# The sample's indexer on both halves of the partitions, its head sums in one bank

## The chip, the cores and the metric

The program runs on one core of a Trainium2 chip. The metric is the device time of one execution in microseconds (us), the median of three runs: 1997.98 us before (1997.33 to 1998.3). The engines are called by their names in the profile: PE (TensorE's products), PEld (its weight loads), DVE (VectorE), ACT (ScalarE), POOL (GpSimd) and SP, whose queue issues nearly all DMAs.

## The reference, cut to what matters

One layer of a decoder for two groups of requests with shared weights: a prompt of 1024 tokens, and a sample of 8 sequences with 8 new tokens each and 512 past keys in pages of 128. The indexer scores each key for each token; the best ones are then attended. The change touches only the indexer of the sample:

```
def select_attend(q, qi, wi, q_pos, k_all, v_all, ki_all):
    ...
    dots = jnp.einsum('bthd,bld->bthl', qi.astype(jnp.float32), ki_all.astype(jnp.float32))
    score = jnp.einsum('bth,bthl->btl', wi.astype(jnp.float32), jax.nn.relu(dots)) * IDX_SCALE
    score = jnp.where(causal[None], score, -jnp.inf)
    _, idx = lax.top_k(score, n_sel)
    ...
```

For one sequence of the sample that is 8 heads x 8 tokens = 64 queries of 64 numbers against 520 keys (512 past, 8 new), a relu, and a weighted sum over the heads, which leaves 8 x 520 scores.

## The kernel before, in words

The whole kernel is one program, written by a planner (the class `Weaver`). The parts of the work are generators ("streams"). The main stream is a long row of projections in fp32r, three products for each 128 x 128 piece of a weight: `pj<-h_hi,wh`, `pj<-h_lo,wh`, `pj<-h_hi,wl`. At each `yield` the planner picks which stream goes on, by its own estimate of each engine's time, so the order of every engine's instructions is fixed when the program is built. A change in one stream moves the others too.

Side streams that run between the projections of the first 350 us:

- `score_stream`: the prompt's indexer, blocks `qb` 2 to 7. A head's chunk of 512 keys is two products (`at<-ki_hi,qstk`, `at<-ki_lo,qstk`), a relu on ACT into one of two buffers (`relu`), and a multiply-add on DVE into `scores` (0.75 us for 512 columns).
- `samp_idx`: the sample's indexer, sequence by sequence. `fetch(b)` reads four page numbers into registers on SP and issues four loads of 128 x 64 keys (`kraw_i`). Four transposes bring them to `pt`, an ACT copy to `kidxT` (64 partitions x 520), and a small DVE copy appends the 8 new keys from `kis`. Two fp32 products of 260 columns (`at<-kidxT,qis`, 64 rows x 64 columns of the array), each with a relu into `srelu`, then two head sums of 260 columns (`at<-srelu,xt`, 64 rows x 8 columns) with an ACT copy each into `sb`, and a DMA of `sb` to its 8 rows of `score_s`. An fp32 product is two PE instructions in the trace.
- `search`: the threshold search on DVE over finished scores, step by step, and after both indexers are done (`scores_done`, the event `ev_go`) the attention of the prompt, `attn`. The sample's own attention, `samp_attn`, follows at about 805 to 905 us.
- `rope` is the rotary step on DVE behind each projection of q, k and the indexer: one product with the cosine table (`rt<-pj,cos`) and two with the sine table (`ru<-pj,sin`); POOL adds the two. Ahead of the first key projection the tables are loaded anew for heads of 128 (`pre_tab(128)`, `load_tabs`): two DMAs of 128 x 1088 floats, `cos<-c_cos` and `sin<-c_sin`, in SP's queue.

Tags are rings of buffers that the planner counts: PSUM banks `pj` (3), `at` (2), `pt` (2), `po` (1); SBUF tiles `M`, `K1`, `Z`, `p`, `S`. An instruction that waits for another engine holds up what the program has behind it on its own.

Of the kernel before, what the change touches and what calls it, by code (L numbers as in the profile page):

```python
# [11 lines left out]
F32 = mybir.dt.float32  # L12
# [16 lines left out]
IH, ID = 8, 64  # L29
PAST, PAGE = 512, 128  # L30
NPG = PAST // PAGE
LS = PAST + NQ
# [22 lines left out]
def n_prompt(c):  # L55
    c0, n = CH[c]
    return min(n, SEQ - c0)
# [258 lines left out]
def hybrid_decoder_step(ctx, tc, I, O):  # L316
    nc = tc.nc
    W = Weaver(nc)
    ctx.enter_context(tc.manual_schedule())

    def dram(shape, dtype, name):
        return tc.dram_tile(shape, dtype, name=name)
# [5 lines left out]
    qis_scr = dram([IH * ID, NS], F32, "qis_scr")  # L328
# [10 lines left out]
    const = ctx.enter_context(tc.tile_pool(name="const", bufs=1))  # L339
# [32 lines left out]
    kis = const.tile([ID, NS], F32, name="kis")  # L372
    ones = const.tile([P, P], F32, name="ones")
    ptab = const.tile([1, NB * NPG], I32, name="ptab")

# [252 lines left out]
    tpool = att.enter_context(tc.tile_pool(name="att", bufs=1, reuse_waits="tile"))  # L628
# [3 lines left out]
    tM = tagged(tpool, "M", 5)  # L632
    tK = tagged(tpool, "K1", 6)
    tZ = tagged(tpool, "Z", 2)
# [215 lines left out]
    def evac_ki(c, ps):  # L850
        c0, n = CH[c]
        npr = n_prompt(c)
        if c == 0:
            st["kh"] = tp_([P, SEQ], F32R, name="ki_hi")
            st["kl"] = tp_([P, SEQ], F32R, name="ki_lo")
        t, u = rope(ps, c, 32, 64)
        W.act(t[64:72, :n], ps[64:72, :n], AF.Copy, n)
        free_ps()
        W.spawn(ki_parts(c, t, u))

    def ki_parts(c, t, u):
# [12 lines left out]
        W.tt(kl[64:128, c0:c0 + npr], t[0:64, :npr], src, OP.subtract, npr)  # L874
        ev_ki[c].t = W.cur.t
        if npr < n:
            W.act(kis, t[0:64, npr:n], AF.Copy, NS)
        W.spawn(ki_out(c, t))

    def ki_out(c, t):  # L880
        yield {"pt": 1, "S": 1}
        ps = psum("pt")
        tl = tok_tiles(c)
        for j, (i, m) in enumerate(tl):
            W.tr(ps[:m, j * 72:(j + 1) * 72], t[:72, j * P:j * P + m], ident[:72, :72])
# [12 lines left out]
        W.later(store)  # L898
# [497 lines left out]
    def pages(b):  # L1396
        W.issue = max(W.issue, W.cur.t) + 2.2
        return [nc.sync.value_load(ptab[0:1, b * NPG + n:b * NPG + n + 1], min_val=0, max_val=I["n_phys"] - 1) for n in range(NPG)]

    def page(cache, v):  # L1400
        return cache[bass.ds(v, 1)].rearrange("o t d -> (o t) d")

    def samp_idx():
        yield ev_wi[2]
        for m in range(4):
            yield ev_qi[m][2]
        yield {"Z": 2, "K1": 1}
        qraw = tZ([ID, IH, NS], name="qis_raw")
        qis = tZ([ID, NB, IH, NQ], name="qis")
        W.load(qraw, qis_scr.rearrange("(h d) t -> d h t", d=ID))  # L1410
        W.go("pool", 2.0)
        nc.gpsimd.tensor_copy(qis.rearrange("p b h q -> p h b q"), qraw.rearrange("p h (b q) -> p h b q", q=NQ))
        W.give("Z")
        xw = tK([NS, IH, NQ], name="xw")
        W.go("dve", 0.2)
        nc.vector.tensor_tensor(xw, wi_c[:NS, 8, :].unsqueeze(2).to_broadcast([NS, IH, NQ]),
                                sdelta.unsqueeze(1).to_broadcast([NS, IH, NQ]), op=OP.mult)
        yield {"pt": 1}
        ps = psum("pt")
        W.tr(ps[:NS, :NS], xw.rearrange("p h q -> p (h q)"), ident[:NS, :NS])  # L1420
        W.give("K1")
        xt = tpool.tile([NS, NS], F32, name="xt")
        W.act(xt, ps[:NS, :NS], AF.Copy, NS)
        W.give("pt")
        yield None
        kr = {}

        def fetch(b):
            yield {"K1": 1}
            kr[b] = tK([P, NPG, ID], name="kraw_i")  # L1430
            t = W.cur.t
            for n, v in enumerate(pages(b)):
                t = W.dma(kr[b][:, n, :], page(I["ckidx"], v))
            kr[b] = (kr[b], t + 3.0)
        yield from fetch(0)
        for b in range(NB):
            if b + 1 < NB:
                yield from fetch(b + 1)
            k_, t = kr.pop(b)
            W.cur.t = max(W.cur.t, t)  # L1440
            yield {"pt": 1, "M": 2}
            ps = psum("pt")
            for n in range(NPG):
                W.tr(ps[:ID, n * P:(n + 1) * P], k_[:, n, :], ident)
            W.give("K1")
            kT = tM([ID, LS], name="kidxT")
            r = tM([NS, LS], name="srelu")
            W.act(kT[:, :PAST], ps[:ID, :], AF.Copy, 512)
            W.give("pt")
            W.ts(kT[:, PAST:LS], kis[:, b * NQ:(b + 1) * NQ], 1.0, None, OP.mult, None, NQ)  # L1450
            yield None
            for a in (0, 260):
                yield {"at": 1}
                ps = psum("at")
                W.mm(ps[:NS, :260], qis[:, b, :, :].rearrange("p h q -> p (h q)"), kT[:, a:a + 260], 260, True, True, f32=True)
                t0 = W.cur.t
                W.act(r[:, a:a + 260], ps[:NS, :260], AF.Relu, 260)
                W.give("at")
                t1, W.cur.t = W.cur.t, t0
            W.cur.t = t1  # L1460
            W.give("M")
            yield {"M": 1}
            sb = tM([NQ, LS], name="sb")
            for a in (0, 260):
                yield {"at": 1}
                ps = psum("at")
                W.mm(ps[:NQ, :260], xt[:, b * NQ:(b + 1) * NQ], r[:, a:a + 260], 260, True, True, f32=True)
                t0 = W.cur.t
                W.act(sb[:, a:a + 260], ps[:NQ, :260], AF.Copy, 260)
                W.give("at")  # L1470
                t1, W.cur.t = W.cur.t, t0
            W.give("M")
            W.cur.t = t1
            yield None
            W.store(score["s"][b * NQ:(b + 1) * NQ, :], sb)
            W.give("M")
        W.give("Z")
        W.cur.t += 2.5
# [577 lines left out]
    M = {}  # L2056
# [419 lines left out]
```

## Time and profile before

| what | value |
|---|---|
| median of three runs | 1997.98 us (1997.33 to 1998.3) |
| the profiled execution: its own time | 1997.44 us |
| its span in the profile | 1995.7 us |
| PE busy | 1944.2 us, 97% of the span |
| DVE, ACT, POOL busy | 64%, 36%, 37% |
| mean granted clock of TensorE | 0.989 |

So 1.74 us of the profiled execution's time lie outside its span, and it is 0.54 us under the median. The shares are averages over stages: PE is full nearly everywhere, DVE is nearly full from about 205 to 500 us and half idle before. A busy share of PE counts a product from its start to its modelled end, and products overlap, so two starts in a row tell more than a duration.

### The profile page before, as it was taken

How to read it: one execution, taken by the hardware profiler on the slowest of the kernel's cores; microseconds unless marked ns; L12 is line 12 of the kernel's file. 1: busy time of each engine (PE TensorE's matmuls, PEld its weight loads, DVE VectorE, ACT ScalarE, POOL GpSimd, SP SyncE). 2: the span in 40 equal slices, each digit the busy share in tenths (PEclk: the TensorE clock that was granted, in tenths of full speed). 3: DMA queues.
4: the chain of work that ended last, by engine and by line, in shares of the span. 5: the costliest groups of instructions: out<-in, count | busy, mean ns of one | idle time of the engine just before them, and what ended most of it. 6: DMA issues, size and time to landing. Idle time of an engine off the chain costs nothing.

```text
span 1995.7 us, 36382 instructions
## 1 busy us (share of the span) xinstructions
PE 1944.2 (97%) x13585; PEld 1864.6 (93%) x13585; DVE 1277.0 (64%) x2727; ACT 713.1 (36%) x1448; POOL 742.7 (37%) x661
## 2 busy tenths in 40 slices
PE   8998999999999999999999899999999999999998
PEld 6987879999999999779999899999999999999988
DVE  6635899899988896323438776566666653314754
ACT  5354443312433325433334532232232322213543
POOL 2533445323223242214444233232232354424873
PEclk9999999999999999999999899999999999999999
DMA  4664325222222222446453332222222343212343
GB/s 151 177 192 110 107 83 151 65 56 73 78 73 55 56 64 72 125 118 187 127 157 113 131 95 86 66 81 81 71 79 79 122 151 106 91 43 85 105 152 96
DMA packets 291243, 205.27 MB, mean 103 GB/s; under 512 B 28448, under 2 KB 270680, under 8 KB 291066
## 3 DMA queue, kind: packets, MB, share of 16 engines
q1 hardware_dynamic: 290822, 202.85, 34.1%
q8 instruction: 107, 1.75, 0.4%
q14 instruction: 70, 0.57, 0.1%
q10 hardware_dynamic: 244, 0.09, 0.0%
HBM read 151.43 MB, written 51.31 MB: 102 GB/s over the span
## 4 chain that ended last, share of the span: by engine, by line
PE 81%; DVE 5%; POOL 2%; issue 2%; DMA 1%; ACT 1%; DVEq 0%; SPq 0%; POOLq 0%; ACTq 0%
PE pj L154 42%; PE pj L190 27%; PE at L186 5%; PE po L186 4%; PE pt L197 3%; POOL wl L150 1%; DVE scores L139 1%; DVE ru L135 0%; DMA q_hi<-ple_scr 0%; POOL x L150 0%; DVE junk L1225 0%; DVE x L135 0%; POOL whl L150 0%; DVE q_lo L135 0%; PE at L197 0%
## 5 line engine op out<-in xcount | busy, mean ns | idle before, releaser
L150 POOL TENSOR_TENSOR wl<-wraw,wh 128x512 fp32r<-128x512 f32 (+2 forms) x233 | 298.9, 1286 | 651.1 <-ACT wh L131 642.1
L190 PE MATMUL pj<-h_hi,wh 128*128 128x384 f32 (+2 forms) x1197 | 406.6, 340 | 0.3 <-ACT wh L131 0.3
L190 PE MATMUL pj<-h_hi,wl 128*128 128x384 f32 (+2 forms) x1197 | 393.6, 329 | 0.7 <-POOL wl L150 0.7
L190 PE MATMUL pj<-h_lo,wh 128*128 128x384 f32 (+2 forms) x1197 | 393.3, 329 | 0.0
L131 ACT ACTIVATE wh<-wraw 128x512 fp32r<-128x512 f32 (+2 forms) x233 | 141.5, 610 | 279.7 <-PE pj L154 137.6
L190 PEld LDWEIGHTS pj<-h_hi,wh 128*128 128x128 f32 (+1 forms) x1197 | 225.9, 189 | 16.3 <-issue 12.4
L190 PEld LDWEIGHTS pj<-h_lo,wh 128*128 128x128 f32 (+1 forms) x1197 | 226.1, 189 | 2.5
L190 PEld LDWEIGHTS pj<-h_hi,wl 128*128 128x128 f32 (+1 forms) x1197 | 225.4, 188 | 1.8 <-POOL wl L150 1.1
L154 PE MATMUL pj<-f_hi,whl 128*128 128x272 f32 x1056 | 206.0, 288 | 0.0
L154 PE MATMUL pj<-f_hi,wl 128*128 128x272 f32 x704 | 203.6, 289 | 0.5 <-DVE wl L135 0.5
L154 PE MATMUL pj<-f_hi,wh 128*128 128x272 f32 x704 | 203.3, 289 | 0.0
L154 PE MATMUL pj<-f_lo,wh 128*128 128x272 f32 x704 | 202.6, 288 | 0.0
L154 PE MATMUL pj<-m_hi,wh 128*128 128x272 f32 x644 | 186.2, 289 | 1.0 <-ACT tha L131 0.5
L154 PE MATMUL pj<-m_hi,wl 128*128 128x272 f32 x644 | 185.9, 289 | 0.0
L154 PE MATMUL pj<-m_lo,wh 128*128 128x272 f32 x644 | 185.8, 289 | 0.0
L135 DVE TENSOR_TENSOR x<-pj,x 128x272 f32<-128x272 f32 x160 | 69.5, 437 | 173.6 <-PE pj L154 170.5
L154 PEld LDWEIGHTS pj<-f_hi,whl 128*128 128x128 f32 x1056 | 168.8, 189 | 0.0
L154 PE MATMUL pj<-f_lo,whl 128*128 128x272 f32 x528 | 152.4, 289 | 0.0
L154 PEld LDWEIGHTS pj<-f_hi,wl 128*128 128x128 f32 x704 | 132.9, 189 | 0.7 <-DVE wl L135 0.7
L154 PEld LDWEIGHTS pj<-f_hi,wh 128*128 128x128 f32 x704 | 132.8, 189 | 0.0
L154 PEld LDWEIGHTS pj<-f_lo,wh 128*128 128x128 f32 x704 | 132.7, 189 | 0.0
L154 PEld LDWEIGHTS pj<-m_hi,wh 128*128 128x128 f32 x644 | 121.4, 188 | 1.5 <-ACT tha L131 0.8
(364 smaller groups left out, 4566.9 us busy)
## 6 DMA issues: line engine op xcount, KB each, us to landing
wraw<-in_w_in SPq DMA_DIRECT2D x112, 256.0 KB
wraw<-in_w_gate_up SPq DMA_DIRECT2D x92, 256.0 KB
wraw<-in_w_down SPq DMA_DIRECT2D x40, 256.0 KB
wraw<-in_w_out SPq DMA_DIRECT2D x32, 256.0 KB
wraw<-in_w_ple_gate SPq DMA_DIRECT2D x32, 256.0 KB
x<-in_x_prompt SPq DMA_DIRECT2D x13, 512.0 KB
m_scr<-q_hi SPq DMA_DIRECT2D x18, 272.0 KB
q_lo<-m_scr SPq DMA_DIRECT2D x18, 272.0 KB
```

Source lines behind the costliest of these rows:

```text
L131: self.nc.scalar.activation(out, in_, func, **kw)
L135: self.nc.vector.tensor_tensor(out, a, b, op=op)
L139: self.nc.vector.scalar_tensor_tensor(out, a, s, b, op0=op0, op1=op1)
L150: self.nc.gpsimd.tensor_tensor(out, a, b, op=op)
L154: self.nc.tensor.matmul(ps, l, r, start=start, stop=stop)
L186: self.nc.tensor.matmul(ps, l, r, start=start, stop=stop)
L190: self.nc.tensor.matmul(ps, l, r, start=start, stop=stop)
L197: self.nc.tensor.transpose(ps, in_, ident)
```

## The change

The sample's keys are laid on all 128 partitions: transposes of two pages at a time (128 x 128) put pages 0 and 1 on partitions 0 to 63 and pages 2 and 3 on partitions 64 to 127 (the page order in `kraw_i` is changed for that), so `kidxT` is 128 x 264, with the 8 new keys behind both halves (`kis` and the queries `qis` now stand on both halves, too). The two fp32 products of a sequence now have 264 columns each and different quarters of the array: rows and columns 0 to 63, and rows and columns 64 to 127. They write the two halves of one `at` bank, and one relu takes both. The weights of the head sum, `xt`, are spread with zeros to 64 columns for each sequence (a POOL memset and two ACT copies, once), so that the sums of all eight sequences add up in one `po` bank, `acc`, by quarters as before; it is copied to `score_s` once at the end by two ACT copies. The copies to `sb` and the eight DMAs to `score_s` are gone.

```diff
@@ ki_parts
         if npr < n:
-            W.act(kis, t[0:64, npr:n], AF.Copy, NS)
+            for e in range(2):
+                W.act(kis[e * ID:(e + 1) * ID, :], t[0:64, npr:n], AF.Copy, NS)
@@ samp_idx
-        W.load(qraw, qis_scr.rearrange("(h d) t -> d h t", d=ID))
+        for e in range(2):
+            W.load(qraw[e * ID:(e + 1) * ID], qis_scr.rearrange("(h d) t -> d h t", d=ID))
...
+        xt = tZ([P, NB * NS], name="xt")
+        W.go("pool", 0.7)
+        nc.gpsimd.memset(xt, 0.0)
...
-            for n, v in enumerate(pages(b)):
-                t = W.dma(kr[b][:, n, :], page(I["ckidx"], v))
+            for i, v in enumerate(pages(b)):
+                t = W.dma(kr[b][:, i % 2 * 2 + i // 2, :], page(I["ckidx"], v))
...
+        yield {"po": 1}
+        acc = psum("po")
         for b in range(NB):
...
-            for n in range(NPG):
-                W.tr(ps[:ID, n * P:(n + 1) * P], k_[:, n, :], ident)
+            for i in range(2):
+                W.tr(ps[:, i * P:(i + 1) * P], k_[:, 2 * i:2 * i + 2, :].rearrange("p n d -> p (n d)"), ident)
...
-            W.act(kT[:, :PAST], ps[:ID, :], AF.Copy, 512)
+            W.ts(kT[:, PAST // 2:], kis[:, b * NQ:(b + 1) * NQ], 1.0, None, OP.mult, None, NQ)
+            W.act(kT[:, :PAST // 2], ps[:, :256], AF.Copy, 256)
             W.give("pt")
-            W.ts(kT[:, PAST:LS], kis[:, b * NQ:(b + 1) * NQ], 1.0, None, OP.mult, None, NQ)
+            yield {"at": 1}
+            ps = psum("at")
+            for e in range(2):
+                s = slice(e * ID, (e + 1) * ID)
+                W.mm(ps[s, :LH], qis[s, b, :, :].rearrange("p h q -> p (h q)"), kT[s, :], LH, True, True, f32=True)
+            W.act(r, ps[:, :LH], AF.Relu, LH)
+            W.give("at")
             yield None
-            for a in (0, 260):
-                yield {"at": 1}
-                ps = psum("at")
-                W.mm(ps[:NS, :260], qis[:, b, :, :].rearrange("p h q -> p (h q)"), kT[:, a:a + 260], 260, True, True, f32=True)
...
-                W.mm(ps[:NQ, :260], xt[:, b * NQ:(b + 1) * NQ], r[:, a:a + 260], 260, True, True, f32=True)
...
-                W.act(sb[:, a:a + 260], ps[:NQ, :260], AF.Copy, 260)
...
-            W.store(score["s"][b * NQ:(b + 1) * NQ, :], sb)
+            for e in range(2):
+                s = slice(e * ID, (e + 1) * ID)
+                W.mm(acc[s, :LH], xt[s, b * NS:(b + 1) * NS], r[s, :], LH, b == 0, b == NB - 1, f32=True)
+            W.give("M", 2)
+        yield None
+        W.act(score["s"][:, 0:PAST // 2], acc[:NS, :PAST // 2], AF.Copy, 256)
+        W.act(score["s"][:, PAST // 2:LS], acc[NS:, :LH], AF.Copy, LH)
```

The instruction order moves from about 120 us on, where the sample's indexer begins, up to the end of the sample's attention at about 905 us. From there to the end PE, DVE, ACT, POOL and SP have the same rows in the same order as before. Three places of the new order matter below. In the rows a matmul is one row with its columns, without the two passes of fp32; x2 is two in a row.

On PE, sequence 5 before (the prompt's indexer, projections and the sample's products take turns):

```order
L186 MATMUL at<-ki_lo,qstk 128x384
L186 MATMUL at<-kidxT,qis 64x260
L190 MATMUL pj<-h_hi,wh 128x384
L190 MATMUL pj<-h_lo,wh 128x384
L190 MATMUL pj<-h_hi,wl 128x384
L190 MATMUL pj<-h_hix,wh 128x384
L190 MATMUL pj<-h_lox,wh 128x384
L190 MATMUL pj<-h_hix,wl 128x384
L186 MATMUL at<-ki_hi,qstk 128x512
L186 MATMUL at<-ki_lo,qstk 128x512
L186 MATMUL at<-kidxT,qis 64x260
```

and after:

```order
L186 MATMUL at<-ki_hi,qstk 128x512
L186 MATMUL at<-ki_lo,qstk 128x512
L186 MATMUL at<-kidxT,qis 64x264 x2
L186 MATMUL at<-ki_hi,qstk 128x384
L186 MATMUL at<-ki_lo,qstk 128x384
```

The two products of a sequence, which stood apart there, now stand together; so do its two head sums.

On PE at the first key projection (`pt<-ident,rt` are the transposes of its rotary result, `x_keep`'s are `pt<-ident,x`), sequence 1 before, whose sequence 0 is already through:

```order
L186 MATMUL at<-kidxT,qis 64x260 x2
L190 MATMUL pj<-h_hi,wh 128x384
L190 MATMUL pj<-h_lo,wh 128x384
L190 MATMUL pj<-h_hi,wl 128x384
L190 MATMUL pj<-h_hix,wh 128x384
L190 MATMUL pj<-h_lox,wh 128x384
L190 MATMUL pj<-h_hix,wl 128x384
L197 MATMUL pt<-ident,rt 128x128 x3
L197 MATMUL pt<-ident,x 128x128 x4
L186 MATMUL at<-srelu,xt 8x260
```

and after, where sequence 0 comes to the same place:

```order
L197 MATMUL pt<-ident,kraw_i 128x128 x2
L190 MATMUL pj<-h_hi,wh 128x384
L190 MATMUL pj<-h_lo,wh 128x384
L190 MATMUL pj<-h_hi,wl 128x384
L190 MATMUL pj<-h_hix,wh 128x384
L190 MATMUL pj<-h_lox,wh 128x384
L190 MATMUL pj<-h_hix,wl 128x384
L197 MATMUL pt<-ident,rt 128x128 x3
L186 MATMUL at<-kidxT,qis 64x264 x2
```

The whole of sequence 0 (but its transposes) and what sequence 1 had done have moved behind the transposes of the rotary result.

On DVE at the same place, before (the first `rt<-pj,cos` here is the first that needs the new tables):

```order
L139 SCALAR_TENSOR_TENSOR scores<-relu,wi_c,scores 128x512 x7
L135 TENSOR_TENSOR scores<-scores,b_112 128x128
L144 TENSOR_SCALAR kidxT<-kis 64x8
L135 TENSOR_TENSOR rt<-pj,cos 128x384
L135 TENSOR_TENSOR ru<-pj,sin 64x384 x2
L144 TENSOR_SCALAR kidxT<-kis 64x8
```

and after:

```order
L139 SCALAR_TENSOR_TENSOR scores<-relu,wi_c,scores 128x512 x4
L135 TENSOR_TENSOR rt<-pj,cos 128x384
L135 TENSOR_TENSOR ru<-pj,sin 64x384 x2
L139 SCALAR_TENSOR_TENSOR scores<-relu,wi_c,scores 128x512 x3
L135 TENSOR_TENSOR scores<-scores,b_112 128x128
L144 TENSOR_SCALAR kidxT<-kis 128x8
```

Three multiply-adds of the prompt's scores and the first key copy, which stood ahead of the rotary step, now stand behind it.

## Rows read from the trace of the kernel before

**Rows 1.** The page, part 1: busy us (share of the span) and instructions.
```profile
PE 1944.2 (97%) x13585; PEld 1864.6 (93%) x13585; DVE 1277.0 (64%) x2727; ACT 713.1 (36%) x1448; POOL 742.7 (37%) x661
```
**Rows 2.** By stretch: length, busy us of PE, PEld, DVE, ACT, POOL; clock, DMA.
```profile
140.00:160.00 20.00, 16.83 (x78) 11.56 (x77) 4.14 (x10) 7.07 (x16) 4.27 (x5) 0.83 0.68 198
...
205.00:360.00 155.00, 145.96 (x816) 130.50 (x815) 144.21 (x335) 58.34 (x131) 73.78 (x76) 0.98 0.39 114
360.00:500.00 140.00, 140.00 (x873) 139.79 (x872) 129.68 (x347) 38.09 (x84) 42.10 (x51) 1.00 0.25 65
```
**Rows 3.** PE's waits from 100 to 360 us: total, times, longest.
```profile
PE at L186 <- ACT relu L131: 7.2, 6, 2.3
PE at L186 <- DVE kidxT L144: 4.1, 2, 3.2
```
**Rows 4.** Timeline of PE around one sequence's products and head sums: start, duration.
```profile
214.37 0.31 PE L190 MATMUL pj<-h_hix,wl 128*128 128x320 f32 x1
214.60 1.09 PE L186 MATMUL at<-kidxT,qis 64*64 64x260 f32 x4
215.62 0.44 PE L190 MATMUL pj<-h_hi,wh 128*128 128x384 f32 x1
215.90 0.33 PE L190 MATMUL pj<-h_lo,wh 128*128 128x384 f32 x1
216.07 0.34 PE L190 MATMUL pj<-h_hi,wl 128*128 128x384 f32 x1
...
216.88 1.04 PE L186 MATMUL at<-srelu,xt 64*8 64x260 f32 x4
217.85 0.44 PE L190 MATMUL pj<-h_hi,wh 128*128 128x384 f32 x1
```
**Rows 5.** Timeline of PE: one product alone, and what follows it.
```profile
225.59 0.65 PE L186 MATMUL at<-kidxT,qis 64*64 64x260 f32 x2
226.16 0.44 PE L190 MATMUL pj<-h_hi,wh 128*128 128x384 f32 x1
```
**Rows 6.** Timeline of PE: the transposes of one sequence's pages.
```profile
189.24 0.60 PE L197 MATMUL pt<-ident,kraw_i 128*64 128x128 f32 x4
189.59 0.42 PE L190 MATMUL pj<-h_hi,wh 128*128 128x384 f32 x1
```
**Rows 7.** Timeline of PE: fp32 products of the sample's attention, two column groups by turns.
```profile
824.06 1.07 PE L186 MATMUL at<-kT,qsmp 128*32 128x260 f32 x8
825.07 0.44 PE L190 MATMUL pj<-h_hi,wh 128*128 128x384 f32 x1
```
**Rows 8.** Timeline of PE at the first key projection.
```profile
152.15 1.12 PE L186 MATMUL at<-kidxT,qis 64*64 64x260 f32 x2 [3.17 <-DVE kidxT L144]
...
154.66 0.52 PE L190 MATMUL pj<-h_lox,wh 128*128 128x384 f32 x1
154.97 0.52 PE L190 MATMUL pj<-h_hix,wl 128*128 128x384 f32 x1
155.29 0.84 PE L197 MATMUL pt<-ident,rt 128*128 128x128 f32 x3
```
**Rows 9.** Timeline of DVE at the same place.
```profile
139.53 0.75 DVE L139 SCALAR_TENSOR_TENSOR scores<-relu,wi_c,scores 128x512 f32<-128x512 f32 x1 [1.13 <-ACT relu L131]
...
149.42 0.56 DVE L135 TENSOR_TENSOR rt<-pj,cos 128x384 f32<-128x384 f32 x1 [8.74 <-PE at L186]
150.78 1.12 DVE L135 TENSOR_TENSOR ru<-pj,sin 64x384 f32<-64x384 f32 x2 [0.80 <-DMA qstk<-qi_scr]
```
**Rows 10.** Timeline of POOL: its addition behind that rotary step.
```profile
152.14 0.99 POOL L150 TENSOR_TENSOR rt<-rt,ru 128x384 f32<-128x384 f32 x1 [6.40 <-DVE kidxT L144]
```
**Rows 11.** Timeline of SP's queue ahead of the tables.
```profile
120.92 0.55 SPq L163 DMA_DIRECT2D x_scr<-xT  x1
...
127.64 6.30 SPq L163 DMA_DIRECT2D kraw_i<-in_cache_kidx  x8
...
143.43 0.68 SPq L163 DMA_DIRECT2D cos<-c_cos  x1
```

More of the change, by code (lines that the diff above doesn't have):

```diff
@@ L371, in hybrid_decoder_step @@
     uc = const.tile([P, KT, 18], F32, name="uc")
-    kis = const.tile([ID, NS], F32, name="kis")
+    kis = const.tile([P, NS], F32, name="kis")
     ones = const.tile([P, P], F32, name="ones")
@@ L1407, in samp_idx @@
         yield {"Z": 2, "K1": 1}
-        qraw = tZ([ID, IH, NS], name="qis_raw")
-        qis = tZ([ID, NB, IH, NQ], name="qis")
-        W.load(qraw, qis_scr.rearrange("(h d) t -> d h t", d=ID))
+        qraw = tZ([P, IH, NS], name="qis_raw")
+        qis = tZ([P, NB, IH, NQ], name="qis")
+        for e in range(2):
+            W.load(qraw[e * ID:(e + 1) * ID], qis_scr.rearrange("(h d) t -> d h t", d=ID))
         W.go("pool", 2.0)
@@ L1413, in samp_idx @@
         W.give("Z")
[L1414 to L1418, printed above, removed]
+        xw = tK([NS, 2, IH, NQ], name="xw")
+        for e in range(2):
+            W.go("dve", 0.2)
+            nc.vector.tensor_tensor(xw[:, e], wi_c[:NS, 8, :].unsqueeze(2).to_broadcast([NS, IH, NQ]),
+                                    sdelta.unsqueeze(1).to_broadcast([NS, IH, NQ]), op=OP.mult)
+        yield {"pt": 1, "Z": 1}
+        xt = tZ([P, NB * NS], name="xt")
+        W.go("pool", 0.7)
+        nc.gpsimd.memset(xt, 0.0)
         ps = psum("pt")
-        W.tr(ps[:NS, :NS], xw.rearrange("p h q -> p (h q)"), ident[:NS, :NS])
+        W.tr(ps[:, :NS], xw.rearrange("p e h q -> p (e h q)"), ident[:NS, :NS])
         W.give("K1")
-        xt = tpool.tile([NS, NS], F32, name="xt")
-        W.act(xt, ps[:NS, :NS], AF.Copy, NS)
+        n = (NB - 1) * (NS + NQ)
+        W.act(xt[:, :n].rearrange("p (b x) -> p b x", x=NS + NQ)[:, :, 0:NQ],
+              ps[:, :NS - NQ].rearrange("p (b q) -> p b q", q=NQ), AF.Copy, NS)
+        W.act(xt[:, n:n + NQ], ps[:, NS - NQ:NS], AF.Copy, NQ)
         W.give("pt")
@@ L1431, in fetch @@
             t = W.cur.t
-            for n, v in enumerate(pages(b)):
-                t = W.dma(kr[b][:, n, :], page(I["ckidx"], v))
+            for i, v in enumerate(pages(b)):
+                t = W.dma(kr[b][:, i % 2 * 2 + i // 2, :], page(I["ckidx"], v))
             kr[b] = (kr[b], t + 3.0)
+        LH = PAST // 2 + NQ
         yield from fetch(0)
+        yield {"po": 1}
+        acc = psum("po")
         for b in range(NB):
@@ L1442, in samp_idx @@
             ps = psum("pt")
-            for n in range(NPG):
-                W.tr(ps[:ID, n * P:(n + 1) * P], k_[:, n, :], ident)
+            for i in range(2):
+                W.tr(ps[:, i * P:(i + 1) * P], k_[:, 2 * i:2 * i + 2, :].rearrange("p n d -> p (n d)"), ident)
             W.give("K1")
-            kT = tM([ID, LS], name="kidxT")
-            r = tM([NS, LS], name="srelu")
-            W.act(kT[:, :PAST], ps[:ID, :], AF.Copy, 512)
+            kT = tM([P, LH], name="kidxT")
+            r = tM([P, LH], name="srelu")
@@ L1449, in samp_idx @@
+            W.ts(kT[:, PAST // 2:], kis[:, b * NQ:(b + 1) * NQ], 1.0, None, OP.mult, None, NQ)
+            W.act(kT[:, :PAST // 2], ps[:, :256], AF.Copy, 256)
             W.give("pt")
-            W.ts(kT[:, PAST:LS], kis[:, b * NQ:(b + 1) * NQ], 1.0, None, OP.mult, None, NQ)
-            yield None
-            for a in (0, 260):
-                yield {"at": 1}
-                ps = psum("at")
-                W.mm(ps[:NS, :260], qis[:, b, :, :].rearrange("p h q -> p (h q)"), kT[:, a:a + 260], 260, True, True, f32=True)
[L1456 to L1466, printed above, removed]
-                W.mm(ps[:NQ, :260], xt[:, b * NQ:(b + 1) * NQ], r[:, a:a + 260], 260, True, True, f32=True)
-                t0 = W.cur.t
-                W.act(sb[:, a:a + 260], ps[:NQ, :260], AF.Copy, 260)
-                W.give("at")
-                t1, W.cur.t = W.cur.t, t0
@@ L1472, in samp_idx @@
-            W.give("M")
-            W.cur.t = t1
-            yield None
-            W.store(score["s"][b * NQ:(b + 1) * NQ, :], sb)
-            W.give("M")
-        W.give("Z")
-        W.cur.t += 2.5
+            yield {"at": 1}
[4 more added lines that the diff above has]
+            W.act(r, ps[:, :LH], AF.Relu, LH)
@@ L1479, in samp_idx @@
+            W.give("at")
+            yield None
+            for e in range(2):
+                s = slice(e * ID, (e + 1) * ID)
[4 more added lines that the diff above has]
+        W.act(score["s"][:, PAST // 2:LS], acc[NS:, :LH], AF.Copy, LH)
+        W.give("po")
+        W.give("Z", 2)
         W.tt(score["s"][:, PAST:LS], score["s"][:, PAST:LS], smask, OP.add, NQ)
```

## The prediction

> **What bounds the kernel now.** The page comes first: PE is busy for 1944.2 us, 97% of the span [rows 1]. The reader is to see that time taken from PE is worth having, and that a mean over the span doesn't say whether PE is the limit where the change lies. So the stretches come next [rows 2]. The sample's indexer lies between 140 and 360 us. From 140 to 160 us PE is busy for 16.83 of 20 us, at a mean clock of 0.83; DVE works for 4.14 us. From 205 to 360 us PE is busy for 145.96 of 155 us, but so is DVE for 144.21: there two engines run neck and neck. From 360 to 500 us PE has no idle time at all. The list of waits says for whom PE stood still between 100 and 360 us [rows 3]: 7.2 us for relus of the prompt's indexer, which themselves wait for buffers that DVE frees, and 4.1 us for `kidxT`, the small DVE copy of the new keys, 3.2 us of that in one piece. Last comes the timeline around one sequence, which prices what is taken away.
>
> **PE's work, step by step.** A product of the projections starts 0.17 us after the one before it (215.90 to 216.07), with 320 columns 0.15. A sequence's two products of 260 columns are four instructions: 1.02 us from their start to the next projection's [rows 4]. Around them 0.23 and 0.28 us lie between starts in place of 0.15 and 0.17, so changing to this part of the array and back costs 0.19 us more. A whole group costs 1.21 us. The head sums: 217.85 - 216.88 = 0.97, with the same 0.19, 1.16 us. Of a group split in two, a half is 0.57 us [rows 5], with 0.19, 0.76 us; I take 0.72 for half a head sum, less by the same 0.05. The four transposes take 0.35 us [rows 6].
> Counted in the program's order, the products are 5 whole groups and 6 halves, the sums 3 whole and 10 halves: 5 x 1.21 + 6 x 0.76 + 3 x 1.16 + 10 x 0.72 + 8 x 0.35 = 6.05 + 4.56 + 3.48 + 7.20 + 2.80 = 24.1 us.
>
> After, there are 8 groups of each, all whole, and 2 transposes for each 4. What a group costs depends on whether two quarters of the array work at once. The trace before has no pair on different rows. The nearest row is the sample's attention [rows 7]: eight fp32 instructions of 260 columns, for two groups of 32 columns by turns, take 1.01 us, as long as four in one place. So two column groups do run side by side, and their outputs lie in two partition ranges of one bank, as here. By that row a group now costs a half: 0.76 and 0.72 us (264 columns for 260 add 0.02), two transposes 0.18: 8 x 1.70 = 13.6 us. PE saves **10.5 us**. The other bound, quarters one after the other: 8 x (1.21 + 1.16 + 0.18) = 20.4 us, a saving of 3.7. I take the first, because what differs (rows too) only separates the two pairs further.
>
> A rule speaks against that. The Trainium skill, "TensorEngine Tiling (Array Packing)", Restrictions and Gotchas, says that different row tiles can't access the same PSUM bank at a time; here both do, in one `at` bank and in `acc`. By it the saving would be 3.7 us in place of 10.5. No row before has two row tiles in one bank, so the rule stands untested here, as the third rival.
>
> **What the new order costs at the first key projection.** SP issues the table load at 143.43 us [rows 11], and the first rotary step with it starts 6.0 us later, at 149.42 [rows 9]. The sines come last: the step ends at 150.78 + 1.12 = 151.90. Behind it on DVE stands the key copy for which PE waits 3.17 us, to 152.15 [rows 8]; then the clock is half (0.31 us between products in place of 0.17). PE reaches the transposes of the rotary result at 155.29 and does not wait for them.
> After, the work that filled that time is behind those transposes. PE went idle at 152.15 - 3.17 = 148.98. Taken out ahead of that are sequence 0's group (1.21), its sums (1.16), sequence 1's transposes and first product (0.35 + 0.76) and half of sequence 0's transposes (0.17): 3.65 us. Six projections (1.05) are still to come. PE is at the rotary transposes at 148.98 - 3.65 + 1.05 = 146.4. They need the step's end and POOL's addition, 0.99 us [rows 10]: 152.9 if the tables are issued as before. SP's chain ahead of the tables has the same pieces, one weight load less and one query load more, with the page loads (6.30 us) later in it; but the store of `x_scr`, at 120.92 [rows 11], now waits for transposes that stand 18 projections (3 us) later on PE. Between on time and 3 us late I take 1: 153.9. PE then stands idle for 7.5 us in place of 3.2, **4.3 us** more. A second wait follows: three multiply-adds of 0.75 us [rows 9] and the key copy now stand behind the rotary step on DVE, 2.5 us with the small steps, so the copy ends at about 155.4, and sequence 0's products wait 1.0 us beyond the rotary transposes: **1.0 us**. Bounds: nothing, if the tables land early enough that both waits end as before, and 8 us (3 for the late store, 4.3, 1.0), a clock at half for a stretch as before in either case.
>
> **Where DVE limits what PE gains.** Sequence 4 [rows 4] and those behind it fall into 205 to 360 us: 1.21 + 1.16 + 0.35 - 1.70 = 1.0 us for it and 1.52 + 1.44 + 0.35 - 1.70 = 1.6 for each of the three with split groups, 5.8 us of the saving. There DVE has 155 - 144.21 = 10.8 us free. The change takes nothing from DVE, and its key copies keep their size. PE can only use its 5.8 us there if DVE keeps up, by its idle time or by lagging further behind (three `pj` banks). The bounds are 0 and 5.8 us lost; since there is idle time for all of it, but the relu waits show it isn't always where it is wanted, I take **1.0 us**.
>
> **The rest costs nothing.** ACT loses two copies and a relu for each sequence and wins two copies at the end; it is busy for 58.34 of 155 us. POOL's memset, the second query load, the second products of `xw` and copy of `kis` come once, before PE needs them; without that cover they are some 2 us on engines that are half idle. SP loses eight stores, of which each stood at the head of its queue until ACT had copied; the tables are issued before the second of them, so this helps only later loads, and no row before shows PE waiting for those. `acc` holds the only `po` bank until the last sum; its next user is the prompt's attention, which starts after the scores anyway. From 905 us on nothing moves.
>
> **Sum.** -10.5 + 4.3 + 1.0 + 1.0 = -4.2 us against the profiled execution: a span of 1995.7 - 4.2 = 1991.5 and a time of 1997.44 - 4.2 = 1993.2. The median stands 0.54 us above that execution, so the forecast against it is 1997.98 - 4.2 = **1993.8 us**, 0.21% below. A measurement of this kernel can tell about 0.2%, 4 us, from no change, so the forecast lies just outside it.
>
> **Rivals.**
> 1. *The whole saving comes through.* The tables land before PE comes to them, or DVE's lag hides the waits: 1998.0 - 10.5 = 1987.5. For it: PE is full from 360 us on. Against it: the order on PE and DVE above, and DVE's 93% share. Chance 0.18.
> 2. *DVE sets the pace* to 360 us. All that sequences 4 to 7 save is lost: -10.5 + 5.3 + 5.8 = +0.6, 1998.6. For it: DVE's 144.21 of 155. Against it: PE waits for relus only 7.2 us in all. Chance 0.15.
> 3. *The quarters work one after the other.* -3.7 + 5.3 = +1.6 and DVE limits nothing: 1999.6, no measurable change. For it: the skill's rule. Against it: rows 7. Chance 0.10.
> 4. *Slower: the tables are late.* The cosine load stands behind a store that waits for PE's later transposes and behind the page loads; each us that it slips is a us on PE, since nothing is left between. From the sum's -4.2 it takes 8.2 us (an issue at 152.6, with the 1 us counted) to come to +4; the price of a slip of 9 us is +4.8 on no change, 2002.8. Against it: SP's pieces are the same. Chance 0.12.
>
> **How the numbers follow.** The forecast, quarters at once and part of the saving lost, from 1990 to 1996.5, has 0.45. Of it two thirds lie under 1994.0, the bound of 0.2%: faster is 0.30 + 0.18 = 0.48. No change is 0.15 from there, 0.15 from rival 2 and 0.09 from rival 3: 0.39. Slower is 0.12 and what is left of rival 3: 0.13. The range for 8 in 10 runs from 1986.5 (rival 1 and a us) to 1999.6 (rivals 2 and 3); it leaves out rival 4 and a tail below.
>
> **What would show it.** The eight groups `at<-kidxT,qis` of four instructions about 0.57 us from their start to the next product (1.0 means rival 3), the head sums likewise in `po`. At the first key projection one idle time of PE of about 7 us, ended by POOL's addition, with half a clock behind it; if it is 3 us or less, rival 1, if over 15, rival 4. From 205 to 360 us PE's waits for relus about as before; if they grow by 5 us, rival 2. From 905 us on, the same stretches to within half a us. The prediction is wrong above all if a wait appears that no row of before has, for instance in the attention between 300 and 350 us, where the order moved, too.

## The result, and the profile after

The changed kernel takes 2014.16 us in the median (2012.91 to 2016.73) and the kernel before 1997.95 in the same comparison: a ratio of 1.0081, 95% interval 1.0067 to 1.0096, so 16.2 us slower, where 4 us faster was forecast. The profiled execution took 2012.91 us at a span of 2011.1. PE has less to do, as the page's first part says (columns as in [rows 1]):

```profile
PE 1937.9 (96%) x13569; PEld 1864.6 (93%) x13569; DVE 1271.0 (63%) x2728; ACT 705.1 (35%) x1428; POOL 740.3 (37%) x662
```

So the span grew by 15.4 us while PE's busy time fell by 6.3: PE stands still for 21.7 us more. First, what was meant to be saved. The timeline of PE around the last sequence's products and head sums after the change:

```profile
256.25 0.31 PE L190 MATMUL pj<-h_hix,wl 128*128 128x320 f32 x1
256.48 0.66 PE L186 MATMUL at<-kidxT,qis 64*64 64x264 f32 x4
257.08 0.44 PE L186 MATMUL at<-ki_hi,qstk 128*128 128x384 f32 x1
...
259.15 0.66 PE L186 MATMUL po<-srelu,xt 64*64 64x264 f32 x4
259.82 0.50 PE L186 MATMUL at<-ki_hi,qstk 128*128 128x512 f32 x1
```

From the group's start to the next instruction's it is 0.60 us for the products, where a whole group took 1.02 [rows 4], and 0.67 for the sums, where it took 0.97. The two quarters run at once. Added over all eight sequences in the same way, without idle time: products 9.5 us before, 5.4 now; sums 8.7 and 5.3; transposes 2.8 and 1.3. That is 9.0 us less. The steps into and out of a group come on top; they are as wide as before (0.23 and 0.28 us here, as in [rows 4]), but there are 16 groups in place of 24, which saves another 1.3.

Next the stretches and PE's waits of the changed kernel. The first three stretches answer to [rows 2]; of the waits, the last piece, from 100 to 360 us, answers to [rows 3]:

```profile
140.00:160.00 20.00, 13.12 (x73) 11.46 (x71) 7.48 (x12) 5.48 (x12) 5.85 (x5) 0.88 0.65 198
205.00:360.00 155.00, 143.78 (x846) 132.83 (x845) 143.51 (x327) 58.09 (x131) 73.91 (x75) 0.99 0.41 116
360.00:500.00 140.00, 137.65 (x849) 136.50 (x849) 126.52 (x343) 34.85 (x77) 41.92 (x51) 1.00 0.24 61
690.00:760.00 70.00, 63.61 (x375) 62.27 (x374) 59.37 (x125) 16.64 (x31) 23.02 (x23) 0.95 0.25 65
```
```profile
PE pt L197 <- POOL rt L150: 5.1, 1, 5.1
PE pt L197 <- DMA x<-in_x_prompt: 3.5, 1, 3.5
PE at L186 <- DVE kidxT L144: 1.8, 1, 1.8
...
PE at L186 <- ACT relu L131: 7.1, 7, 2.3
PE at L186 <- DVE mx L1295: 4.0, 1, 4.0
...
PE at L186 <- DMA qh<-qh_scr: 4.1, 1, 4.1
PE at L186 <- DVE mx L1295: 2.3, 1, 2.3
PE pt L197 <- POOL psmp L1554: 2.2, 2, 1.9
PE at L186 <- ACT kT L131: 1.2, 1, 1.2
...
PE at L186 <- ACT relu L131: 10.5, 10, 2.3
```

The four pieces of the list are 100 to 160 us, 205 to 360 us, 690 to 860 us and once more 100 to 360 us, of which only the relus are shown. The piece from 690 us lies over 400 us behind the indexer, whose last sum ends at 260 us. What one reads from them: the relu waits have grown from 7.2 to 10.5 us (from 205 to 360 us alone from 5.5 to 7.1), so VectorE holds PE up by some 3 us more, less than the 5 that the prediction named for VectorE setting the pace; the new waits are for a load of x (3.5), for the rotary step (5.1 and 1.8, where it was 3.2), for the maxima of the attention (4.0 and 2.3) and for queries `qh` (4.1).

To place the loss, one counts the products of the projections (`pj`), which are the same 11,656 in both kernels, and compares the start of the same one (us, worked out from the trace; e1 is the first experiment, with the changed instructions in the order of before):

```
product     before    after       e1
    576      163.3    169.1    162.6
   1152      318.9    326.1    312.6
   1536      399.3    399.5    393.7
   2784      667.4    662.5    662.0
   3168      743.7    745.5    738.2
   3360      828.1    838.6    823.1
   3552      905.2    920.1    901.7
   5800     1228.2   1242.9   1224.8
idle time of PE from product 1 to 1536, to 2784, to 3600, to the end
          21.8  0.2  3.7  16.2      31.7  2.3  11.3  17.0      26.9  0.2  3.8  15.6
```

Up to 400 us the changed kernel has saved 9 us of work and stood still for 10 more. From there to 2784 it seems to gain 5, but only because attention work is put off: 108 transposes of `p` lie there instead of 128. Behind 2784 it comes due, with 7.6 us more of idle time than before, and 15 us stay to the end. From product 1536 to 3600 the changed kernel and e1 run the same 3228 PE instructions; they take 528.3 us in the one and 515.6 in the other, and 9.7 of these 12.7 us are idle time. So the put-off work is not more work; what costs is mostly that PE stands.

The late stand, in SP's queue of the changed kernel (start, duration):

```profile
727.24 0.36 SPq L163 DMA_DIRECT2D ql<-ql_scr  x1
728.52 0.36 SPq L163 DMA_DIRECT2D qh<-qh_scr  x1
729.77 1.81 SPq L163 DMA_DIRECT2D wraw<-in_w_in  x2
745.86 0.37 SPq L163 DMA_DIRECT2D ql<-ql_scr  x1
749.15 0.37 SPq L163 DMA_DIRECT2D qh<-qh_scr  x1
```

From 731.6 to 745.9 SP stands at a load of `ql`, whose buffer (`K1`) the search's tiles `eq`, `z` and `lob` hold in turn, until POOL has added the last long piece of the bias at 744.69 + 1.15 us. In the order of before (e1) three pairs of queries are under way before that:

```profile
715.84 0.37 SPq L178 DMA_DIRECT2D ql<-ql_scr  x1
717.13 0.36 SPq L178 DMA_DIRECT2D qh<-qh_scr  x1
...
725.21 0.50 SPq L178 DMA_DIRECT2D ql<-ql_scr  x1
725.80 0.42 SPq L178 DMA_DIRECT2D qh<-qh_scr  x1
726.97 0.36 SPq L178 DMA_DIRECT2D ql<-ql_scr  x1
727.42 0.42 SPq L178 DMA_DIRECT2D qh<-qh_scr  x1
```

And the stretch 690 to 760 us is full there, at the whole clock, 5.7 us of PE more than in the changed kernel's row above:

```profile
690.00:760.00 70.00, 69.33 (x427) 66.88 (x427) 58.72 (x129) 21.12 (x40) 25.32 (x25) 1.00 0.25 66
```

### The profile page after: what moved, and what is told of

It is laid out like the page before. It is cut to its first block, busy times and chain, and to the rows that moved or that the text cites. A ratio compares the mean times of both kernels' runs of the same rounds, so it can differ in the third digit from the quotient of the medians.

```text
span 2011.1 us, 36314 instructions
## 1 busy us (share of the span) xinstructions
PE 1937.9 (96%) x13569; PEld 1864.6 (93%) x13569; DVE 1271.0 (63%) x2728; ACT 705.1 (35%) x1428; POOL 740.3 (37%) x662
## 4 chain that ended last, share of the span: by engine, by line
PE 77%; DVE 9%; issue 2%; POOL 2%; DMA 1%; ACT 1%; SPq 0%; DVEq 0%; ACTq 0%; POOLq 0%
PE pj L154 43%; PE pj L190 24%; PE po L186 4%; PE at L186 3%; PE pt L197 2%; DVE scores L139 1%; DVE junk L1226 1%; DVE ru L135 1%; DVE cum L1262 1%; DVE cv L139 0%; DVE rt L135 0%; DVE eq L146 0%; POOL x L150 0%; DMA q_hi<-ple_scr 0%; DMA q<-ple_scr 0%
## 5 line engine op out<-in xcount | busy, mean ns | idle before, releaser
L190 PEld LDWEIGHTS pj<-h_hi,wh 128*128 128x128 f32 (+1 forms) x1197 | 226.8, 189 | 10.1 <-issue 5.7
```

The lines of the kernel that those rows point to most:

```text
L190: self.nc.tensor.matmul(ps, l, r, start=start, stop=stop)
```

## The experiments

**Theory:** the changed instructions save what they should; what costs time is that the planner, whose clocks they move, writes another order of all the rest, and that order has stands which the one before had not. **Rival 1:** the changed instructions themselves bring the loss. **Rival 2:** PE's saving is waited away in any order.

### Instructions and order, crossed (e1, e2)

e1 emits the changed instructions where the old ones stood, and charges the planner the old costs; e2 does the opposite. `W.plan` charges and emits nothing, `nc` emits and charges nothing. In e1, for instance:

```
             for a in (0, 260):
                 yield {"at": 1}
-                ps = psum("at")
-                W.mm(ps[:NS, :260], qis[:, b, :, :]..., kT[:, a:a + 260], 260, True, True, f32=True)
+                if a == 0:
+                    ps = psum("at")
+                    for e in range(2):
+                        s = slice(e * ID, (e + 1) * ID)
+                        nc.tensor.matmul(ps[s, :LH], qis[s, b, :, :]..., kT[s, :], start=True, stop=True)
+                    nc.scalar.activation(r, ps[:, :LH], AF.Relu)
+                else:
+                    at_plan()      # W.cur.t = max(W.cur.t, W.take("at"))
+                W.plan(W.mm, None, None, None, 260, True, True, f32=True)
```

> The changed instructions (halved keys, paired products, one bank of sums) are put at the places that the old ones had, and the planner is charged the old costs, so that on every engine all other rows stand in the order of the kernel before. Theory (the planner's other order cost the time, the instructions themselves saved it): the paired products and transposes take some 9 us less of PE, and the waits of 3.5 us at 126 us, 5.1 us at 151 us and 4.1 us at 747 us are not there: 1987 to 1993 us. Rival 1 (the instructions themselves bring the loss, by a lower clock or slower evictions): 2008 to 2016 us. Rival 2 (VectorE sets the pace of 205 to 360 us, and the saving of PE is waited away): 1996 to 1999 us.

> The opposite: the old instructions of the sample's indexer (whole keys, whole products, sums of each sequence stored by SP), put where the changed ones stand, with the planner charged the changed costs, so that all other rows stand in the order of the changed kernel. Theory (order costs, instructions save): the changed kernel's 2014 us and the 9 us of PE on top, 2019 to 2026 us. Rival 1 (the instructions themselves bring the loss): 1995 to 2002 us. Rival 2 (PE's saving is waited away in either order): 2011 to 2016 us.

e1: 1993.58 us, ratio 0.998 (0.9966 to 0.9993), 0.6 us above the theory's range and 2.4 below that of rival 2. e2: 2023.3 us, ratio 1.0132 (1.0111 to 1.0153), within the theory's. The ratios are to runs of the kernel before that were made alongside. Those scatter from 1991 to 2005 us and their medians from 1997.3 to 2000.1, so 2 or 3 us between runs made at different times tell nothing. In the traces every other instruction of e1 stands in the order of the kernel before, and every other one of e2 in that of the changed kernel. So in the old order the changed instructions give 4.8 us by the medians, in the new order 9.1 (2023.3 to 2014.2); the order costs 25 us with the old instructions and 20.6 with the changed ones. Rival 1 falls. Rival 2 falls as it was put, since a gain is left in both orders, but in e1 about half of the saving is waited away. Where, its waits say, from 100 to 160 us and from 205 to 360 us:

```profile
PE at L1492 <- DVE kidxT L1481: 6.2, 1, 6.2
...
PE at L201 <- ACT relu L146: 4.9, 4, 2.1
PE po L201 <- DVE ptl L150: 2.8, 1, 2.8
PE pt L212 <- POOL p L1322: 1.5, 1, 1.5
```

The one wait of 6.2 us was 3.2 [rows 8]: VectorE stands for the table, in its timeline, and SP issued that load at 142.50 us.

```profile
149.13 0.56 DVE L150 TENSOR_TENSOR rt<-pj,cos 128x384 f32<-128x384 f32 x1 [9.29 <-DMA cos<-c_cos]
```

### Other orders of the same instructions (e5 to e8)

```
-        W.go("pool", 2.0)
+        W.go("pool", 0.6)     # e5 and e7; 3.0 in e6 and e8
         nc.gpsimd.tensor_copy(qis.rearrange("p b h q -> p h b q"), ...)
```

This is a charge in the planner's books and no instruction. e5 and e6 have it in the kernel before, e7 and e8 in the changed one.

> The kernel before with one number of the planner changed: the charge for GpSimd's copy of qis, 2.0 to 0.6 us, which is what the trace shows for it (603 ns). No instruction changes, but the order on TensorE moves as far as in the change itself. Theory (any edit that touches the planner's clocks throws the order anew, and orders differ by ten us and more): off by over 4 us from 1998 in either direction, 1990 to 2025 us. Rival (orders are worth much the same, and the change's order is bad for a reason of its own, such as the bank and the two buffers that it holds till its end): 1995 to 2001 us.

> The same number of the planner at 3.0 us instead of 2.0 in the kernel before. Theory (orders scatter): off by over 4 us from 1998 in either direction, and not where the charge of 0.6 lies, 1990 to 2025 us. Rival (the change's order is bad for a reason of its own): 1995 to 2001 us.

> The changed kernel with the same number at 0.6 instead of 2.0 us; only the order moves. Theory (orders scatter): off by over 4 us from 2014, anywhere from 1985 to 2020 us, rather below than above, since 2014 is 20 us over what the changed instructions gave in the old order. Rival (the change's bank and buffers held till the end make any order of it bad): 2010 to 2018 us.

> The changed kernel with the same number at 3.0 instead of 2.0 us. Theory (orders scatter): off by over 4 us from 2014, 1985 to 2020 us. Rival (any order of the changed kernel is bad): 2010 to 2018 us.

Before: 2013.16 us at 0.6 (ratio 1.008, 1.0059 to 1.0101) and 2013.47 at 3.0 (1.0079, 1.0061 to 1.0096). Changed: 2000.1 at 0.6 (1.0014, 1.0001 to 1.0026) and 2007.64 at 3.0 (1.0046, 1.0028 to 1.0064). The two orders of before came out together, against that part of the expectation for e6, but both are 15 us off the kernel before, with its instructions to the letter. Four orders each, then: old instructions 1998, 2013, 2013 and 2023 us, changed ones 1994, 2000, 2008 and 2014. The order of the kernel before is the best of its four, and the change drew the worst of its own. The means are 2012 and 2004, but with such a scatter four draws can't show a difference of 8; that the instructions are better is shown by the two pairs in one order, e1 and e2. None of the three orders that the planner itself wrote for the changed instructions (2000, 2008, 2014) beats the kernel before.

The late stand comes with an order and not with the change. PE's waits from 690 to 860 us in e6, whose instructions are those of before:

```profile
PE at L186 <- DMA qh<-qh_scr: 5.5, 1, 5.5
PE at L186 <- DVE mx L1294: 2.3, 1, 2.3
```

### The stands, one by one, in the changed order (e3, e4)

e3 gives the search's tiles buffers of their own (`z` and `lob` in the same way as `eq` below), e4 puts the stores of `x_scr` on ScalarE's queue; the planner books the same as before, so all else keeps its place.

```
-                eq = tK([P, 512], BF, name="eq")[:m, :n]
+                eq = (W.take("K1"), tpool.tile([P, 512], BF, tag="E1", name="eq", bufs=3)[:m, :n])[1]
...
+            nc.scalar.dma_start(x_scr[:, :, i * P:i * P + m], o[:, :, :m])
             def store(i=i, m=m, o=o):
-                W.store(x_scr[:, :, i * P:i * P + m], o[:, :, :m])
+                W.plan(W.store, x_scr[:, :, i * P:i * P + m], o[:, :, :m])
```

> The changed kernel in its own order, but the three tiles of the top-k bias (eq, z, lob) have a buffer of their own and no longer share one with the queries of the attention, so that the loads of ql and qh at 732 to 749 us need not wait for the end of the search. Theory (this stand of SP is one of the three places of the loss): the 4.1 us wait at 747 us goes, the half clock after it too, and some of the attention's deferral: 2003 to 2010 us. Rival (PE only waits for something else there, the scores of the search or VectorE): 2012 to 2016 us.

> The changed kernel in its own order, but the stores of the transposed x go out on ScalarE's queue, right behind the copy that makes the tile, so that SP does not stand for them and loads the next x tile earlier. Theory (the stand of SP at 116 to 124 us and the late x tile at 126 us are one of the three places): the 3.5 us wait and the 3.4 us at half clock behind it go, 2008 to 2011 us. Rival (the time comes back as a longer wait at the first key projection at 151 us, which waits for VectorE and POOL): 2012 to 2016 us.

e3: 2006.62 us, ratio 1.0047 (1.0032 to 1.0062). The wait for `qh` is gone from its list from 690 to 860 us; one for the maxima stays:

```profile
PE at L186 <- DVE mx L1295: 3.2, 2, 2.4
PE pt L197 <- POOL psmp L1554: 2.2, 2, 1.9
```

By the medians that is 7.5 us, by the spans of the two profiled executions (2007.9 and 2011.1) 3.2; the ratios, 1.0047 and 1.0081, say 6.8. The stand costs 3 to 7.5 us.

e4: 2009.58 us, ratio 1.0064 (1.004 to 1.0089), 4.6 us less by the medians and 3.4 by the ratios, whose intervals overlap. In the changed kernel SP stood as its timeline shows (the last row is the table, for later), and PE behind it:

```profile
115.22 0.57 SPq L163 DMA_DIRECT2D out_new_v_prompt<-to  x1
124.18 0.55 SPq L163 DMA_DIRECT2D x_scr<-xT  x1
124.82 0.62 SPq L163 DMA_DIRECT2D x<-in_x_prompt  x1
...
145.77 0.48 SPq L163 DMA_DIRECT2D cos<-c_cos  x1
```
```profile
126.40 0.27 PE L197 MATMUL pt<-ident,xw 64*128 64x64 f32 x1
130.15 1.06 PE L197 MATMUL pt<-ident,x 128*128 128x128 f32 x8 [3.47 <-DMA x<-in_x_prompt]
```

In e4 that wait is 0.8 us, but the next one has grown from 5.1 to 8.5: PE's waits from 100 to 160 us.

```profile
PE pt L212 <- POOL rt L165: 8.5, 1, 8.5
PE at L201 <- DVE kidxT L159: 1.8, 1, 1.8
PE pt L212 <- DMA x<-in_x_prompt: 0.8, 1, 0.8
```

So e4 is 3.8 us ahead of the changed kernel at product 480 (131.6 against 135.4), the late table takes half of that back, 1.9 at product 576 (167.2 against 169.1), and 3.4 us are left from product 3552 on. So the theory's range held, and its rival's mechanism, a longer wait at the key projection, was there too. The stands follow one another: what one releases, the next partly keeps.

### The tables of the key projection (e9, e10, e12, then e13, e14)

The tables get buffers of their own and are loaded on ScalarE's queue behind the first group (e9, e10, e12) or before the first value group, some 100 us into the kernel (e13, e14). e9 and e12 are e1 and the kernel before with that alone; e10, e13 and e14 have the x stores of e4 too (e10 and e13 on e1, e14 on the kernel before).

```
+            if i == 3:
+                for nm in ("cos", "sin"):
+                    tab2[nm] = tpool.tile([P, T], F32, name=nm + "2")
+                    nc.scalar.dma_start(tab2[nm], I[f"c_{nm}128"])
             yield from run_group(gr)
```

> The changed instructions in the old order (as in the run of 1993.6 us), and the two tables of the key projection in buffers of their own, loaded on ScalarE's queue right after the first group instead of by SP at 142.5 us. Every other row keeps its place. Theory (the 6.2 us for which TensorE stands at 146 us come from the late table, which VectorE waits for, and are what the saved products ran into): the stand and the half clock behind it go, 1985 to 1990 us. Rival (VectorE's and POOL's work from 150 us on sets the pace, and the time is waited later): 1991 to 1995 us.

> As the run with the early tables, and the stores of the transposed x on ScalarE's queue as well. In the old order SP does not stand for them long, so theory: 0 to 2 us less than with the early tables alone, 1984 to 1990 us. Rival (ScalarE's queue pays for issuing them): 1 to 3 us more.

> The kernel before, with the early tables alone. Theory (its stand at the first key projection is 3.2 us): 3 to 5 us less than before, 1993 to 1995 us, and the distance to the changed instructions in the same order with the same early tables is then 6 to 9 us instead of 4.8, since the products' saving no longer runs into the table. Rival (no gain): 1997 to 1999 us, distance 5 us.

e9: 1989.42 us, ratio 0.9958 (0.9943 to 0.9973). e10: 1987.27, 0.9954 (0.9938 to 0.9969). e12: 1997.66, 0.9999 (0.9987 to 1.0011). e9 and e10 lie in their theories' ranges. By the medians the changed instructions are now worth 8.2 us in the same order (e12 to e9) where they were worth 4.8, but the intervals of these differences overlap, and the traces don't say the same: product 1300 starts 4.8 us earlier in e9 than in e12, and 5.6 earlier in e1 than in the kernel before. So that the saving had run into the late table is not shown. That e12 gained nothing was the rival's, but not for its reason. Its wait at the key projection is gone, and another came, as PE's waits from 60 to 160 us show:

```profile
PE pt L212 <- DMA sraw<-in_state_conv: 4.1, 1, 4.1
```

The load of the state lay behind the bytes of the tables; in the kernel before PE waits 0.9 us there. So the tables were loaded later:

> As the run of 1987.3 us (changed instructions, old order, early tables, x stores on ScalarE's queue), but the tables are loaded before the first value group, some 100 us into the kernel, where no load is waited for. Theory (the wait of 4.4 us at 68 us for the state came from the tables' bytes ahead of it): it falls to the 0.9 us of before, 1981 to 1985 us. Rival (the time comes back at the key projection or in VectorE's waits): 1986 to 1990 us.

> The kernel before with the same two repairs (tables before the first value group, x stores on ScalarE's queue). Theory (its stand at the key projection cost 3.2 us and half clock behind it): 1991 to 1995 us, 8 to 11 us above the changed instructions with the same repairs, which is then what the change's instructions are worth when nothing stands in their way. Rival (the change's saving is eaten elsewhere): 4 to 6 us above.

e13: 1985.74 us, ratio 0.9927 (0.9914 to 0.9939), a little above the theory's range and below its rival's; the wait for the state is back at 0.9 us, and of its 3.5 us, 1.5 came through by the medians (5 by the ratios). e14: 1993.41, 0.9969 (0.9955 to 0.9982), as expected. The same waits in e13, complete, hold no table and no x any more:

```profile
PE at L201 <- ACT relu L146: 1.7, 1, 1.7
PE pt L212 <- DMA sraw<-in_state_conv: 0.9, 1, 0.9
PE pt L212 <- ACT vt L146: 0.9, 1, 0.9
```

e13 beats both kernels, by 0.7% and 1.4%; by the medians the changed instructions have 7.7 us of it (e14 to e13), just short of the 8 to 11 that were expected (8.4 by the ratios); by the traces it is 4.9 at product 1300 and 5.0 between the spans (1988.9 and 1983.9).

### All repairs in the changed order (e11, e15)

> The changed kernel in its own order with all three repairs: tables early on ScalarE's queue, x stores on ScalarE's queue, own buffers for the tiles of the top-k bias. Theory (the order's loss sits in these three stands of SP's queue, 3.5, 5.1 and 4.1 us of TensorE, and the half clock behind each): 2014 less 14 to 18 us, 1996 to 2000 us. Rival (each repair gives back part of its gain at the next wait, since VectorE and POOL are as late as before): 2002 to 2008 us.

> The changed kernel in its own order with the three repairs, the tables loaded before the first value group. Theory: 1999.6 us of the earlier version less the 4 us at 68 us, 1993 to 1997 us, which leaves 10 to 14 us between its order and the old one with no stand of SP's queue left before 700 us. Rival (given back at the next wait): 1998 to 2001 us.

Both are the changed kernel with the repairs of e3 and e4 and the tables, early in e11 and later in e15. e11: 1999.62 us, ratio 1.0008 (0.9996 to 1.0021), within the theory's range. e15: 1997.76, 0.9989 (0.9977 to 1.0001), just above it; of the 4 us that the state's wait had cost e11, 2 came through by the medians and nearly all by the ratios. Repairing three stands of SP's queue was thus worth 16 us, as much as the change had lost. But two of the repairs help the old order too, by 7.8 us with the changed instructions (e1 to e13; 10.6 by the ratios) and by 6.2 with the old ones (e14, by its ratio). So of the some 20 us between the two orders the repairs take away only some 8, and 12 still lie there with the same instructions (e15 to e13). By the count of products, all of it arises behind product 1536, which starts at 386.2 us in e15 and at 387.4 in e13; product 3552 starts at 905.2 and 894.8. From product 1536 to 3600, with the same 3228 PE instructions, e15 takes 526.6 us and e13 515.2: PE is idle for 10.2 us in place of 3.9, and the other 5.1 us are instructions that start further apart.

## Why the prediction failed, by its steps

**PE's saving, 10.5 us:** right, in kind and in size. The 10.5 hold 0.19 us for the steps into and out of each group, 24 before and 16 after, which is 1.5; the 9.0 measured above are without these steps, and 10.3 with them. In e1 it is 9.4 and 10.4. Rival 3 is out: 0.60 us for four instructions in place of 1.02. The rule weighed with it (the Trainium skill, "TensorEngine Tiling (Array Packing)", Restrictions and Gotchas: different row tiles can't access one PSUM bank at the same time) is not borne out here as a cost of time; the measurement decides. Each pair here differs in its columns, too; row tiles alone no run tried.

**The first key projection, 4.3 and 1.0 us more:** right in kind, too large by 1.6. In the changed kernel the stands are 5.1 and 1.8 where 7.5 and 1.0 were expected, 3.7 us more than the 3.2 before; the cosine load goes out at 145.77 us, 2.3 us later than [rows 11], where 1 was taken. In the old order it is 6.2 for 3.2, 3.0 us more. Whether the term could be had back is another matter. With early tables the stand is gone, and by the medians the changed instructions gain 7.7 to 8.2 us instead of 4.8; by the traces they gain some 5 us either way, since more is then waited for VectorE.

**VectorE's limit, 1.0 us:** too small. In e1, the idle time between products 528 and 1400 beside the key projection's grew by 2.1. With the stand gone, PE is idle there for 15.6 us in e13 and 10.1 in e14, so some 5.5 us of the saving is waited away, near the bound of 5.8; the waits for relus are 10.3 us in e13 and 6.7 in e14 (142 to 362 us). The two terms were added up, but the second takes over what the first lets go.

**The rest costs nothing:** this is the step that failed. For the changed instructions it holds: in e1 the distance to before is 5.6 us at product 1300 and 5.4 at 3200; 1.9 are lost around 850 us, in the sample's attention, where the granted clock is at half for a stretch that the trace of before has not (a mean of 0.76 from 838 to 842 us). For the order it does not. The prediction followed the moved instructions to the first key projection and took every place behind it to be as before, though the same comparison of the two orders showed them apart up to 905 us. It named a wait "that no row of before has" as what would make it wrong, and put no price and no chance on it: its 0.13 for slower stood nearly all for late tables. The missing term is 20 us of order (20.6, e1 to the changed kernel): by the traces 5.8 up to product 1536 and 12.7 from there to 3600, mostly idle time of PE. The x load, the table and the buffers of the search account for some 8 of it, what the repairs give the new order beyond the old; for the other 12 the runs show where they lie and not what makes them.

**The sum:** 1993.8 us was forecast and 1993.58 measured in e1, for the change without its new order. That agreement is partly luck: the saving was right, but in e1 the key projection cost 3.0 in place of 5.3, VectorE's limit 2.1 in place of 1.0, and the sample's attention 1.9 in place of nothing.

**From 905 us on nothing moves:** right; the distance is 14.9 us at product 3552 and 14.7 at 5800.

**What stays open:** why the planner, with its books changed by so little, writes this order and not another was not followed through its choices; the runs show only that a charge of another value does the same. Of e15's last 12 us, 6.3 are seen as idle time and 5.1 as wider steps between the same instructions; what causes either was not taken apart. Whether the changed instructions are worth 5 us in the old order, as the traces say, or 8 without the late table, as the medians say, is open as well.

## What to carry to other kernels

Where a planner's clocks write the order, an edit is two changes: the instructions, and a new draw of the order. Time the instructions alone, in the old order, and draw a few orders of the kernel before by a charge that emits nothing, to know how far they scatter (here 25 us), before believing either a gain or a loss below that. A saving on the busiest engine is worth only what the next wait lets through, here about half: look for the late transfer and for the engine that is nearly as full (VectorE, 144 of 155 us), and don't add up two waits that can stand in for each other. When a load is moved forward, look for what its bytes push back.

## What was not expected of the hardware

A VectorE operation of 64x8 elements took 2.56 us while POOL worked through two tiles, in the middle of the late stand (timelines of DVE and POOL in the changed kernel):

```profile
746.04 2.56 DVE L146 TENSOR_SCALAR eq<-score_s,candb 64x8 bf16<-64x8 f32 x1
```
```profile
744.69 1.15 POOL L150 TENSOR_TENSOR score_s<-z,lob 64x512 f32<-64x512 bf16 x1 [3.77 <-DVE lob L146]
...
746.07 2.52 POOL L150 TENSOR_TENSOR wl<-wraw,wh 128x512 fp32r<-128x512 f32 x2
```

It ends at 748.60 and POOL's pair at 748.59. The next load of `qh`, for which PE waits 4.1 us, goes out at 749.15, when the step behind it that reads `eq` (`z`, 748.91 to 749.13) has ended. The Trainium skill, "SBUF — State Buffer", SBUF: two separate sides, says that VectorE in some of its modes and GpSimd take a shared pair of ports in turn, each for a whole instruction; this row agrees with it, for two instructions of POOL in a row. The orders of the other runs make a test of it, though none was made for that: in e5, with POOL idle, the same operation takes 0.22 us; in e7 and e8, beside one instruction of POOL, 0.60 and 0.62; in the other traces, beside two, 1.86 to 2.60; and each time but in e5 it ends 0.02 to 0.03 us behind an instruction of POOL. In the kernel before it is 1.87.
